# Two products with ones for each norm's sum, root and reciprocal by columns, and a reload spread between products: a decoder layer on one Trainium2 core

## The chip, the cores and the metric

The kernel runs on one core of one Trainium2 chip. Five engines work from queues of their own: TensorE (PE, matrix products into the eight PSUM banks), VectorE (DVE), ScalarE (ACT), GpSimd (POOL) and SyncE (SP, which here issues most DMAs). The metric is the device time of one execution in microseconds (us), a median over runs. The profile calls the loading of weights into PE "PEld".

## The reference

One layer of a hybrid decoder on 1024 prompt tokens and 8 sequences of 4 new tokens (1056 tokens in all), float32, width 1024:

```python
def _rms(x, g):
    return x * lax.rsqrt(jnp.mean(x * x, axis=-1, keepdims=True) + EPS) * g

def _layer(x, p, ...):
    h = _rms(x, n_mix_pre)
    z = h @ w_in                      # q, k, v, pooling input
    a, k_state, v_state = attn_fn(q, k, v)
    m, pool_state = _pool_mixer(u, pool_prev, pos0, w_pool, pool_scale)
    x = x + _rms(concat([a, m]) @ w_out, n_mix_post)
    f = _rms(x, n_ffn_pre)
    f = (silu(f @ w_gate) * (f @ w_up)) @ w_down
    x = x + _rms(f, n_ffn_post)
    x = x + sigmoid(x @ w_ple_gate) * (p @ w_ple)
```

There are four norms per layer. Each needs, for every token, the sum of 1024 squares.

## The kernel before

**Layout.** Activations lie with features on the 128 partitions and tokens along the columns. The 1056 tokens are three groups of N = 352 columns; a half of a group is a tile of 128 x (4 x 352). Every float32 product is made of three single-pass products: each operand is split into a rounded high part and a low part (`split`, L171 to L174: a cast on ACT, then a subtraction on DVE), and high x high, high x low and low x high are added in a PSUM bank. The slots of the pool for activations (30) and of the raw weights (3) are reused; a tile waits until the last reader of its slot is done.

**The norm.** Squares are added over the eight chunks of features into `acc`, 128 x 352. What is left is the sum over the partitions, then 1/sqrt(sum/1024 + eps), and that value on all partitions for the multiplications that follow. `rstd_steps` (L355 to L384) does this twelve times: one pre-mix norm for each group (through `u_norm`, which copies the result to SBUF, L546), two in `ffn_steps` (the norm after mixing and the one before the FFN) for each group, and one in `x2_steps` (after the FFN) for each group. It makes three small products of `acc` with a column of ones (L363, the sums then stand by tokens on partitions), takes root (L365) and reciprocal (L366) of 128 x 3, splits it (L368, L369), multiplies a constant band of identity tiles `diag` by both parts (L375, `dg`) and makes two products with a matrix of ones (L383), which leave the value of each token on all partitions of a PSUM bank.

**The FFN.** Groups 0 and 1 are treated together by a scheme of seven products of half blocks (`seven`, `do_dn_pair`), group 2 directly (`do_one`, `do_dn_one`). The gate and up weights come in slabs of four pairs; the down products of a slab (`do_dn_pair`, two steps j = 0, 1, of seven products with two banks each) add into `accp` on DVE (`ap`, L1226). Group 2's normalised input is used early for the first slabs, then spilled to DRAM (`fsd`), and read back by `do_reload` ahead of the last slab's down products: two halves `fr` by DMA (L1251), each then split into `fh` and `fl`. It is used again from the direct products behind `do_combine`.

**Order.** The program is written by a planner in Python. `STEPS` lists the product steps. Side work such as norms and operand splits is written as generators, which are put on a list with `chain`; each product calls `turn(n)`, n being its matmuls, and `turn` moves the generators on when their time has come. A generator's `yield load, wait` says how many units of DVE work it has just issued (divided by a `share`) and how many units to wait more. `finish` runs generators to their end on the spot. The order of PE is then fixed as written; the order on the other engines is set by a scheduler that follows it. Each engine works through its queue in order.

Of the kernel before, what the change touches and what calls it, by code (L numbers as in the profile page):

```python
# [10 lines left out]
F32 = mybir.dt.float32  # L11
F32R = mybir.dt.float32r
AF = mybir.ActivationFunctionType
ALU = mybir.AluOpType
AX = mybir.AxisListType

P = 128
D = 1024
# [7 lines left out]
N = T // G  # L26
# [1 line left out]
OFF = tuple(N * g for g in range(G + 1))  # L28
NX = N

TB = 3
WIN = 128
NB = SEQ // WIN
PW = (2, 4, 8, 16)
# [28 lines left out]
def trunk_kernel(  # L63
# [32 lines left out]
    nc = tc.nc  # L96
    te, ve, se, ge = nc.tensor, nc.vector, nc.scalar, nc.gpsimd
# [4 lines left out]
    spool = ctx.enter_context(tc.tile_pool(name="spool", bufs=2))  # L102
# [5 lines left out]
    def nm(s):  # L108
        cnt[0] += 1
        return f"{s}{cnt[0]}"  # L110

    def act_tile(shape, dt=F32, s="a"):
        return apool.tile(shape, dt, tag="a", bufs=A_SLOTS, name=nm(s))

    def half(g, dt=F32, s="h"):
        return act_tile([P, 4, NS[g]], dt, s)
# [9 lines left out]
    def mm(*args, **kw):  # L126

        ins = te.matmul(*args, **kw)  # L128
        if pinned[0]:
            tc.keep_in_program_order(ins)  # L130

    def bank():
        return psum.tile([P, 512], F32, tag="b", name=nm("b"))
# [4 lines left out]
    def const(shape, src=None, s="c", dt=F32):  # L138
        t = cpool.tile(shape, dt, name=nm(s))
        if src is not None:  # L140
            nc.scalar.dma_start(t, src)
        return t
# [3 lines left out]
    ident = const([P, P])  # L146
    make_identity(nc, ident)

    diag = const([P, TB, P])
    lap = TB * P - N  # L150
    for i in range(TB - 1):
        ge.tensor_copy(diag[:, i, :], ident)
    ge.memset(diag[:, TB - 1, :], 0.0)
    ge.tensor_copy(diag[:, TB - 1, : P - lap], ident[:, lap:])
    ones = const([P, P])
    ge.memset(ones, 1.0)
    ones_r = const([P, P], dt=F32R)
    ge.tensor_copy(ones_r, ones)
    epst = const([P, 1])
# [7 lines left out]
    def fix(ins):  # L167

        if fixed[0]:
            tc.keep_in_program_order(ins)  # L170

    def split(hi, lo, src):
        fix(se.copy(hi, src))  # L173
        fix(ve.tensor_tensor(lo, src, hi.bitcast(F32), op=ALU.subtract))  # L174
# [140 lines left out]
    def need(k, ahead=LOOK):  # L315

        for i in range(len(made), min(k + ahead + 1, len(ITEMS))):
            kind, js = ITEMS[i]
            if kind == "direct":
                w_split(js[0])  # L320
                made[i] = pairs[js[0]]
            elif kind == "half":
                w_load(js[0])
                hl = two_in_one([P, 4, P])
                split(*hl, raws[js[0]][:, 4:8, :])
                made[i] = hl
            elif kind == "small":
                w_load(js[0])
                hl = two_in_one([P, 2, 256])
                split(*hl, raws[js[0]])  # L330
                made[i] = hl
            else:
                made[i] = w_sums(*(raws[ITEMS[j][1][0]] for j in js))
            for kind, js in ITEMS[i + 1 : i + 3]:
                if kind != "sums":
                    w_load(js[0])
        return made[k]
# [17 lines left out]
    def rstd_steps(acc):  # L355

        n = acc.shape[1]
        sm = bank()  # L360
        for i in range(TB):
            at = min(i * P, n - P)
            mm(sm[:, i : i + 1], acc[:, at : at + P], ones[:, 0:1], start=True, stop=True)  # L363
        sd = spool.tile([P, TB], F32, tag="sd", name=nm("sd"))
        fix(se.activation(sd, sm[:, :TB], AF.Sqrt, bias=epst, scale=1.0 / D))  # L365
        fix(ve.reciprocal(sd, sd))  # L366
        hl = spool.tile([P, 2, TB], F32R, tag="hl", name=nm("hl"))
        fix(ve.tensor_copy(hl[:, 0], sd))  # L368
        fix(ve.tensor_tensor(hl[:, 1], sd, hl[:, 0].bitcast(F32), op=ALU.subtract))  # L369
        dgs = []  # L370
        dg2 = act_tile([P, 2, TB, P], F32R, "dg")
        for h in range(2):
            dg = dg2[:, h]
            fix(
                ve.tensor_tensor(  # L375
                    dg, diag, hl[:, h].bitcast(F32).unsqueeze(2).to_broadcast([P, TB, P]), op=ALU.mult
                )
            )
            dgs.append(dg.rearrange("p i k -> p (i k)"))
        yield 6, 14  # L380
        ps = bank()
        for h in range(2):
            mm(ps[:, :n], ones_r, dgs[h][:, :n], start=h == 0, stop=h == 1)  # L383
        return ps[:, :n]  # L384

    def acc_rows():
        t = act_tile([P, 4, NX], s="acc")
        return [t[:, g, : NS[g]] for g in range(G)]
# [30 lines left out]
    xs, acc1, r1 = [[None] * 2 for _ in range(G)], acc_rows(), [None] * G  # L419
# [77 lines left out]
    n = 4 * NDEC * PST  # L497
# [44 lines left out]
    def u_norm(steps, g):  # L542
        try:
            next(steps)
        except StopIteration as e:
            fix(se.copy(acc1[g], e.value))  # L546
            r1[g] = acc1[g]

    pinned[0] = True
    norms = [None] * G  # L550
# [95 lines left out]
    for c in range(4):  # L646
        n = NDEC * DSEQ
# [67 lines left out]
    def scores(b):  # L715


        t = act_tile([P, 8, WIN])
        cur = [bank() for _ in range(2)]
        prv = [bank() for _ in range(2)] if b else None  # L720
        for c in range(4):
            for which, at in ((cur, b), (prv, b - 1)):
                if which is None:
                    continue
                for kv in range(2):
                    rows = slice(64 * kv, 64 * kv + 64)
                    mm(
                        which[kv][:, c * WIN : (c + 1) * WIN],
                        qT[c][rows, b * WIN : (b + 1) * WIN],
                        kT[rows, at * WIN : (at + 1) * WIN],  # L730
                        start=True,
                        stop=True,
                    )
        for kv in range(2):
            tk = t[:, 4 * kv : 4 * kv + 4, :]
            if b:
                se.copy(tk, v4(prv[kv]))
                ve.copy_predicated(tk, m4(0).bitcast(mybir.dt.int32), v4(cur[kv]))
            else:
                ve.tensor_tensor(tk, v4(cur[kv]), m4(1), op=ALU.add)  # L740
            hs = slice(4 * kv, 4 * kv + 4)
            softmax(tk, 4, 0.125, skp[:, hs], nskp[:, hs])
        return t
# [98 lines left out]
    acc = acc_rows()  # L842
# [46 lines left out]
    t = scores(order[0])  # L889
# [16 lines left out]
    for a, b in zip(order, order[1:] + [None]):  # L906
# [11 lines left out]
        t = t2  # L918
# [10 lines left out]
    fs = [None, None, []]  # L929
# [5 lines left out]
    chains = []  # L935
# [16 lines left out]
    def chain(steps, wait=0, alone=False):  # L952

        chains.append([steps, now[0] + wait, alone])

    def finish(ch_list):
        for ch in ch_list:
            for _ in ch[0]:
                pass
            chains.remove(ch)  # L960
# [40 lines left out]
    def f_operand(src, g):  # L1001
        hi, lo = half(g, F32R, "fh"), half(g, F32R, "fl")
        split(hi, lo, src)
        return hi, lo
# [4 lines left out]
    fsd = [dpool.tile([P, 4, N], F32, name=nm("fsd")) for _ in range(2)]  # L1009
# [190 lines left out]
    accp = {}  # L1200

    def do_dn_pair(s, j, items):
        if j == 0:
            finish(list(chains))
        ia, ib, is_ = items
        for at, which, h, x in (
            (1, ia, 0, "B11"),
            (2, ia, 1, "B21"),
            (4, ib, None, "T4"),
            (6, is_, "S2", "T2"),  # L1210
            (7, is_, "S3", "T3"),
            (5, is_, "S1", "T1"),
            (3, is_, "S4", "B22"),
        ):
            w = need(which)
            w = w if h is None else w[h] if which == is_ else quarter(w, h)
            xh, xl = h7[x]
            if at not in accp:
                accp[at] = half(0, s="ap")
            for r in range(2):  # L1220
                ps = bank()
                gemm(ps[:, :N], [(w[0][:, 2 * c + r, :], w[1][:, 2 * c + r, :], xh[:, c, :], xl[:, c, :]) for c in range(2)])
                turn(6)
                o = accp[at][:, 2 * j + r, :]
                if s:
                    ve.tensor_tensor(o, o, ps[:, :N], op=ALU.add)  # L1226
                else:
                    se.copy(o, ps[:, :N])

    def do_combine():  # L1230
        for a, b in ((2, 1), (1, 6), (7, 1), (1, 5), (1, 3), (4, 7), (7, 5)):
            ve.tensor_tensor(accp[a], accp[a], accp[b], op=ALU.add)
        os_[0] = [accp[2], accp[4]]
        os_[1] = [accp[1], accp[7]]
        for g in (0, 1):
            begun.update((g, m) for m in range(KC))
# [9 lines left out]
            nc.sync.dma_start(d, t)  # L1246

    def do_reload():
        for h in range(2):
            t = half(2, s="fr")  # L1250
            nc.sync.dma_start(t, fsd[h])  # L1251
            fs[2][h] = f_operand(t, 2)

    def do_reload_sums():
        os_[2] = [half(2, s="o") for _ in range(2)]
# [217 lines left out]
```

## Time and profile before

| | us |
|---|---|
| median of 3 runs | 1093.5 |
| lowest and highest | 1092.64, 1093.7 |
| the profiled execution | 1093.79 |
| its span | 1092.0 |
| its mean granted PE clock | 0.996 |

Twelve norms and the reload are spread over the whole span: the pre-mix norms lie before 55 us, the six of `ffn_steps` between 220 and 340, the reload near 820, the norms after the FFN between 880 and 1010. Page part 2 cuts the span into 40 slices of 27.3 us and gives the busy share of each engine in tenths.

```profile
DVE  6777478886878966796598898999899997969973
ACT  7423276674555533345543443344443364445531
PEclk9999999999999999999999999999998999999999
```

A row of a timeline has the start, the time from the start to the end of the last of a group, the engine, line, operation, output and input, size and count; in brackets, how long the engine had been idle and what released it. A row of the grouped view ends with busy time, mean nanoseconds of one, and idle time before them. A row of the waits has the total, the number and the longest.

### The profile page before, as it was taken

The page shows a single profiled execution, that of the slowest core. Times are in us where ns is not written, and L with a number is a line of the kernel's source. Part 1 is how long each engine was busy: PE and PEld are TensorE (multiplying, and loading weights), DVE is VectorE, ACT ScalarE, POOL GpSimd, SP SyncE. Part 2 cuts the span into 40 slices and gives each one's busy share as a digit, 9 for nine tenths or more (in the row PEclk, how much of TensorE's full clock was granted, in tenths as well). Part 3 has the DMA queues.
Part 4 walks back from the last instruction along what each step waited for, and adds up shares of the span by engine and source line. Part 5 has one row for each costly group of instructions (what it writes and reads, how often), then busy time and mean ns, then how long its engine had stood idle before and what let it go on. Part 6 is the DMA issues. An engine that isn't in the chain of part 4 may idle for free.

```text
span 1092.0 us, 17927 instructions
## 1 busy us (share of the span) xinstructions
PE 1080.0 (99%) x6979; PEld 1063.7 (97%) x6979; DVE 874.5 (80%) x1298; ACT 511.4 (47%) x863; POOL 284.4 (26%) x212
## 2 busy tenths in 40 slices
PE   9999999999999999999999999999998999999998
PEld 8999988899999999999999999999998999999998
DVE  6777478886878966796598898999899997969973
ACT  7423276674555533345543443344443364445531
POOL 0073032200000023435445454455442000022400
PEclk9999999999999999999999999999998999999999
DMA  8121311544553432322222212213224545553351
GB/s 295 59 71 39 120 48 40 179 150 136 190 186 131 135 116 77 131 78 78 82 74 83 91 59 94 81 59 115 74 88 179 172 167 213 189 209 130 126 203 60
DMA packets 43573, 131.29 MB, mean 120 GB/s; under 512 B 5060, under 2 KB 15588, under 8 KB 43488
## 3 DMA queue, kind: packets, MB, share of 16 engines
q1 hardware_dynamic: 42160, 128.38, 34.4%
q10 hardware_dynamic: 1328, 1.77, 0.5%
q8 instruction: 55, 0.90, 0.3%
q14 instruction: 30, 0.25, 0.1%
HBM read 114.25 MB, written 15.87 MB: 119 GB/s over the span
## 4 chain that ended last, share of the span: by engine, by line
PE 91%; DVE 4%; DMA 2%; issue 1%; ACT 1%; POOL 1%; SPq 0%; DVEq 0%; POOLq 0%; ACTq 0%
PE b L128 90%; PE b L122 1%; DMA xr<-in_x_dram 1%; DMA a<-in_dmask_dram 1%; POOL wr L1054 1%; DVE sl L174 0%; SPq L402 0%; DVE wl L174 0%; DVE mx L693 0%; ACT xr L436 0%; DVE a L801 0%; ACT wh L173 0%; DVE hf L1129 0%; DVE h L428 0%; ACT h L426 0%
## 5 line engine op out<-in xcount | busy, mean ns | idle before, releaser
L1054 POOL TENSOR_TENSOR wr<-wr,wr 128x512 f32<-128x512 f32 x108 | 175.0, 1636 | 484.3 <-DMA wr<-in_w_gu_dram 217.3
L173 ACT CAST wh<-wr 128x1024 fp32r<-128x1024 f32 (+1 forms) x138 | 142.1, 1031 | 165.7 <-PE b L128 99.4
L174 DVE TENSOR_TENSOR wl<-wr,wh 128x1024 fp32r<-128x1024 f32 (+1 forms) x138 | 169.1, 1226 | 49.1 <-ACT wh L173 33.9
L128 PE MATMUL b<-fh,wh 128*128 128x352 f32 x624 | 201.5, 323 | 0.0
L128 PE MATMUL b<-fl,wh 128*128 128x352 f32 x624 | 199.9, 320 | 0.0
L128 PE MATMUL b<-fh,wl 128*128 128x352 f32 x624 | 199.9, 320 | 0.0
L173 ACT CAST sh<-wr 128x1024 fp32r<-128x1024 f32 x72 | 75.7, 1051 | 139.2 <-POOL wr L1054 131.5
L128 PE MATMUL b<-fh,sh 128*128 128x352 f32 x416 | 134.3, 323 | 0.0
L128 PE MATMUL b<-fl,sh 128*128 128x352 f32 x416 | 133.2, 320 | 0.0
L128 PE MATMUL b<-fh,sl 128*128 128x352 f32 x416 | 133.2, 320 | 0.0
L174 DVE TENSOR_TENSOR sl<-wr,sh 128x1024 fp32r<-128x1024 f32 x72 | 96.1, 1336 | 36.8 <-ACT sh L173 18.5
L128 PEld LDWEIGHTS b<-fl,wh 128*128 128x128 f32 x624 | 117.3, 188 | 0.0
L128 PEld LDWEIGHTS b<-fh,wh 128*128 128x128 f32 x624 | 117.0, 188 | 0.0
L128 PEld LDWEIGHTS b<-fh,wl 128*128 128x128 f32 x624 | 117.0, 188 | 0.0
L128 PE MATMUL b<-h,wh 128*128 128x352 f32 x480 | 104.9, 324 | 0.9 <-ACT h L426 0.7
L128 PE MATMUL b<-hid,wh 128*128 128x352 f32 x416 | 99.5, 322 | 0.0
L128 PEld LDWEIGHTS b<-h,wh 128*128 128x128 f32 x480 | 81.4, 188 | 2.1 <-DVE h L428 1.0
L128 PE MATMUL b<-hp,sh 128*128 128x352 f32 x320 | 78.3, 328 | 4.7 <-DVE ap L1226 4.0
L1054 POOL TENSOR_TENSOR wr<-wr 128x512 f32<-128x512 f32 x36 | 51.0, 1418 | 106.5 <-DVE w L174 106.5
L128 PEld LDWEIGHTS b<-fl,sh 128*128 128x128 f32 x416 | 78.2, 188 | 0.0
L128 PEld LDWEIGHTS b<-fh,sh 128*128 128x128 f32 x416 | 78.0, 188 | 0.0
L128 PEld LDWEIGHTS b<-fh,sl 128*128 128x128 f32 x416 | 77.9, 187 | 0.0
(195 smaller groups left out, 2253.6 us busy)
## 6 DMA issues: line engine op xcount, KB each, us to landing
wr<-in_w_gu_dram SPq DMA_DIRECT2D x88, 512.0 KB, 3.3
wr<-in_w_dn_dram SPq DMA_DIRECT2D x40, 512.0 KB, 3.2
wr<-in_w_pg_dram SPq DMA_DIRECT2D x16, 512.0 KB, 3.5
x<-in_x_dram SPq DMA_DIRECT2D x6, 704.0 KB, 9.6
x1d<-x SPq DMA_DIRECT2D x6, 704.0 KB, 3.5
x<-x1d SPq DMA_DIRECT2D x6, 704.0 KB, 6.3
out_y_dram<-yo SPq DMA_DIRECT2D x24, 176.0 KB, 2.1
wr<-in_w_out_b_dram SPq DMA_DIRECT2D x8, 512.0 KB, 3.5
```

Source lines behind the costliest of these rows:

```text
L122: ins = te.transpose(out, src, ident)
L128: ins = te.matmul(*args, **kw)
L173: fix(se.copy(hi, src))
L174: fix(ve.tensor_tensor(lo, src, hi.bitcast(F32), op=ALU.subtract))
L1054: ge.tensor_tensor(out, a, b, op=op)
```

## The change

`rstd_steps` splits `acc` itself, 128 x 352, into a high and a low part, multiplies both with the matrix of ones, and so has the sum of every token on all partitions; then ACT takes the root over 352 columns from PSUM and DVE the reciprocal in place. The result stands in SBUF, in `acc`. The small products, the band of identities and the copy in `u_norm` go.

`do_reload` becomes a generator on the list: both DMAs at its first step, then one half's split after 50 units and the second 10/share + 30 units later. The call that finished all generators moves from the first of the last down products to `do_combine` (and so for every slab's `do_dn_pair`).

```diff
-    diag = const([P, TB, P])
...
     def rstd_steps(acc):
         n = acc.shape[1]
-        sm = bank()
-        for i in range(TB):
-            at = min(i * P, n - P)
-            mm(sm[:, i : i + 1], acc[:, at : at + P], ones[:, 0:1], start=True, stop=True)
-        sd = spool.tile([P, TB], F32, tag="sd", name=nm("sd"))
-        fix(se.activation(sd, sm[:, :TB], AF.Sqrt, bias=epst, scale=1.0 / D))
-        fix(ve.reciprocal(sd, sd))
-        hl = spool.tile([P, 2, TB], F32R, tag="hl", name=nm("hl"))
-        fix(ve.tensor_copy(hl[:, 0], sd))
-        fix(ve.tensor_tensor(hl[:, 1], sd, hl[:, 0].bitcast(F32), op=ALU.subtract))
-        dgs = []
-        dg2 = act_tile([P, 2, TB, P], F32R, "dg")
-        for h in range(2):
-            dg = dg2[:, h]
-            fix(
-                ve.tensor_tensor(
-                    dg, diag, hl[:, h].bitcast(F32).unsqueeze(2).to_broadcast([P, TB, P]), op=ALU.mult
-                )
-            )
-            dgs.append(dg.rearrange("p i k -> p (i k)"))
-        yield 6, 14
+        hl = act_tile([P, 2, n], F32R, "hl")
+        split(hl[:, 0], hl[:, 1], acc)
+        yield 4, 14
         ps = bank()
         for h in range(2):
-            mm(ps[:, :n], ones_r, dgs[h][:, :n], start=h == 0, stop=h == 1)
-        return ps[:, :n]
+            mm(ps[:, :n], ones_r, hl[:, h], start=h == 0, stop=h == 1)
+        fix(se.activation(acc, ps[:, :n], AF.Sqrt, bias=epst, scale=1.0 / D))
+        fix(ve.reciprocal(acc, acc))
+        return acc
     def u_norm(steps, g):
...
-            fix(se.copy(acc1[g], e.value))
-            r1[g] = acc1[g]
+            r1[g] = e.value
     def do_dn_pair(s, j, items):
-        if j == 0:
-            finish(list(chains))
     def do_combine():
+        finish(list(chains))
     def do_reload():
-        for h in range(2):
-            t = half(2, s="fr")
-            nc.sync.dma_start(t, fsd[h])
-            fs[2][h] = f_operand(t, 2)
+        def steps():
+            ts = [half(2, s="fr") for h in range(2)]
+            for h in range(2):
+                nc.sync.dma_start(ts[h], fsd[h])
+            yield 0, 50
+            for h in range(2):
+                fs[2][h] = f_operand(ts[h], 2)
+                yield 10, 30
+
+        chain(steps())
```

How the rows move, at three places of DVE. The first is the first norm, at the start: `xr` is the input (squares added up into `acc`, and operand `h` split from it), `a` the first products times the norm's value. Before:

```order
L428 SCALAR_TENSOR_TENSOR h_188<-xr_124,c_72,h_187 128x352 x4
L366 RECIPROCAL sd_335<-sd_335 128x3
L368 CAST hl_338<-sd_335 128x3
L369 TENSOR_TENSOR hl_338<-sd_335,hl_338 128x3
L375 TENSOR_TENSOR dg_341<-c_82,hl_338 128x384 x2
L393 TENSOR_TENSOR xr_120<-xr_120,xr_124 128x1408
L394 TENSOR_TENSOR xr_120<-xr_120 128x704
L395 TENSOR_TENSOR acc_104<-xr_120 128x352
L428 SCALAR_TENSOR_TENSOR h_361<-xr_166,c_72,h_360 128x352 x4
L540 TENSOR_TENSOR a_210<-b_218,acc_104 128x352
```

and of the change:

```order
L405 SCALAR_TENSOR_TENSOR h_183<-xr_119,c_72,h_182 128x352 x4
L167 TENSOR_TENSOR hl_326<-acc_99,hl_326 128x352
L370 TENSOR_TENSOR xr_115<-xr_115,xr_119 128x1408
L371 TENSOR_TENSOR xr_115<-xr_115 128x704
L372 TENSOR_TENSOR acc_99<-xr_115 128x352
L405 SCALAR_TENSOR_TENSOR h_346<-xr_161,c_72,h_345 128x352 x4
L360 RECIPROCAL acc_99<-acc_99 128x352
L405 SCALAR_TENSOR_TENSOR h_391<-xr_194,c_72,h_390 128x352
L517 TENSOR_TENSOR a_205<-b_213,acc_99 128x352
```

Ahead of the product one subtraction stands for five operations; the reciprocal has moved behind it.

The second place is group 2's second FFN norm: `y` its scaled input, `fl` the low part of its operand, `wl` those of weights, `sq` squares of another group. Before:

```order
L366 RECIPROCAL sd_2842<-sd_2842 128x3
L368 CAST hl_2845<-sd_2842 128x3
L369 TENSOR_TENSOR hl_2845<-sd_2842,hl_2845 128x3
L375 TENSOR_TENSOR dg_2848<-c_82,hl_2845 128x384 x2
L978 SCALAR_TENSOR_TENSOR y_1287<-x_2512,c_72,b_2889 128x352 x2
L174 TENSOR_TENSOR wl_2882<-wr_2716,wh_2881 128x1024
L850 TENSOR_TENSOR acc_1301<-acc_1301,sq_2878 128x352
L978 SCALAR_TENSOR_TENSOR y_1287<-x_2512,c_72,b_2889 128x352 x2
L978 SCALAR_TENSOR_TENSOR y_1976<-x_2514,c_72,b_2889 128x352 x2
L174 TENSOR_TENSOR wl_2927<-wr_2885,wh_2926 128x1024
L850 TENSOR_TENSOR acc_1301<-acc_1301,sq_2923 128x352
L978 SCALAR_TENSOR_TENSOR y_1976<-x_2514,c_72,b_2889 128x352
```

and of the change, from the reciprocal to the second half's `fl`:

```order
L360 RECIPROCAL acc_1269<-acc_1269 128x352
L954 SCALAR_TENSOR_TENSOR y_1255<-x_2480,c_72,acc_1269 128x352 x4
L826 TENSOR_TENSOR acc_1269<-acc_1269,sq_2875 128x352
L167 TENSOR_TENSOR wl_2879<-wr_2835,wh_2878 128x1024
L167 TENSOR_TENSOR fl_2885<-y_1255,fh_2884 128x1408
L826 TENSOR_TENSOR acc_1269<-acc_1269,sq_2914 128x352
L167 TENSOR_TENSOR wl_2918<-wr_2837,wh_2917 128x1024
L954 SCALAR_TENSOR_TENSOR y_1944<-x_2482,c_72,acc_1269 128x352 x4
L167 TENSOR_TENSOR wl_2959<-wr_2882,wh_2958 128x1024
L826 TENSOR_TENSOR acc_1269<-acc_1269,sq_2955 128x352
L167 TENSOR_TENSOR fl_2965<-y_1944,fh_2964 128x1408
```

The four scalings of each half now stand together, and the reciprocal heads them where it headed the product before.

The third place is the reload: `p` and `u` are the last gate and up products, `hid` the split of what they make, `ap` the down products' additions. Before:

```order
L1081 TENSOR_TENSOR p_8345<-p_8345,b_8456 128x352
L174 TENSOR_TENSOR fl_8477<-fr_8474,fh_8476 128x1408
L1163 TENSOR_TENSOR u_8421<-u_8421,p_8345 128x352
L174 TENSOR_TENSOR wl_8404<-wr_8343,wh_8403 128x1024
L174 TENSOR_TENSOR hid_8337<-u_8421,hid_8337 128x352
L174 TENSOR_TENSOR w_8486<-wr_8388,w_8486 128x512
L1226 TENSOR_TENSOR ap_5196<-ap_5196,b_8491 128x352
L1226 TENSOR_TENSOR ap_5196<-ap_5196,b_8499 128x352
L1226 TENSOR_TENSOR ap_5213<-ap_5213,b_8507 128x352
```

and of the change, starting with the first addition, which follows `p`:

```order
L1200 TENSOR_TENSOR ap_5116<-ap_5116,b_8399 128x352
L1200 TENSOR_TENSOR ap_5116<-ap_5116,b_8411 128x352
L1139 TENSOR_TENSOR u_8341<-u_8341,p_8265 128x352
L1200 TENSOR_TENSOR ap_5133<-ap_5133,b_8419 128x352
L167 TENSOR_TENSOR wl_8324<-wr_8263,wh_8323 128x1024
L167 TENSOR_TENSOR hid_8257<-u_8341,hid_8257 128x352
L167 TENSOR_TENSOR w_8394<-wr_8308,w_8394 128x512
L1200 TENSOR_TENSOR ap_5133<-ap_5133,b_8427 128x352
L1200 TENSOR_TENSOR ap_5164<-ap_5164,b_8449 128x352
L1200 TENSOR_TENSOR ap_5164<-ap_5164,b_8457 128x352
L1200 TENSOR_TENSOR ap_5185<-ap_5185,b_8471 128x352
L1200 TENSOR_TENSOR ap_5185<-ap_5185,b_8479 128x352
```

The first half's `fl` comes behind these eight additions, the second half's eleven DVE rows later. On SP's queue both `fr` loads now stand together, ahead of one `w_dn` load that used to stand between them.

More of the change, by code (lines that the diff above doesn't have):

```diff
@@ L29 @@
 NX = N
-TB = 3
 WIN = 128
@@ L147, in trunk_kernel @@
     make_identity(nc, ident)
-    diag = const([P, TB, P])
[L150 to L154, printed above, removed]
     ones = const([P, P])
```

## The prediction

> **What bounds the kernel now.** I read the page first: the busy times of the engines.
>
> ```profile
> PE 1080.0 (99%) x6979; PEld 1063.7 (97%) x6979; DVE 874.5 (80%) x1298; ACT 511.4 (47%) x863; POOL 284.4 (26%) x212
> ```
>
> TensorE (PE) is busy for 1080.0 of the span's 1092.0 us. A busy engine is the bound only if it waits for nobody, so the next views are the chain that ended last and the waits of PE.
>
> ```profile
> 218.65 564.72 PE b L128 x3567
> ```
> ```profile
> PE b L128 <- DVE ap L1226: 4.0, 1, 4.0
> ```
>
> The chain's longest pieces are unbroken runs of matmuls; this one (start, length) goes from 218.65 to 783.4. There each pass taken off PE shortens the span by its own time, as long as nothing else gets late. Of the few waits, the longest, 4.0 us at once, is for the down products' additions. The windows show its stage and the one behind it (time, PE, PEld, DVE, ACT, POOL, clock, DMA share, GB/s).
>
> ```profile
> 800.00:830.00 30.00, 25.26 (x148) 24.69 (x147) 26.76 (x39) 14.58 (x20) 12.79 (x8) 0.91 0.45 167
> 830.00:900.00 70.00, 70.00 (x438) 70.00 (x438) 65.66 (x98) 32.71 (x47) 0.23 (x1) 0.99 0.47 160
> ```
>
> In the first, PE loses 4.74 of 30 us, the clock falls to 0.91, and VectorE (DVE) is busy for 26.76: locally DVE is the bound. Behind it PE is full again, but DVE has only 4.3 us left in 70.
>
> **Removed: the 72 passes on the ones column.** Each norm issued three fp32 products of 128x1, two passes each; a timeline of PE shows them as one group of six (start, length).
>
> ```profile
> 226.04 0.72 PE L128 MATMUL b<-c,acc 128*128 128x1 f32 x6
> 226.62 0.41 PE L128 MATMUL b<-mh,wh 128*128 128x352 f32 x1
> 226.87 0.33 PE L128 MATMUL b<-ml,wh 128*128 128x352 f32 x1
> 227.04 0.32 PE L128 MATMUL b<-mh,wl 128*128 128x352 f32 x1
> ```
>
> Starts are what counts here, since passes overlap. A 128x352 matmul normally follows the last after 0.16 us (226.87 to 227.04), so without the six passes the `mh` product would have begun at 226.04 and the `ml` product at 226.20. It began at 226.87: the passes cost 0.67 us, and 12 norms cost 12 x 0.67 = 8.0 us. All lie in stretches where PE waits for nothing, except the first. The two products with ones remain, with data of 352 columns where `dg` stood: no change on PE. **Term 1: -8.0 us.**
>
> **Moved: what precedes the two products.** Before, they wait for a root, a reciprocal, a cast, a subtraction and two products with the diagonal; now for a cast and a subtraction over 352 columns. The nearest rows for these are the hidden layer's split.
>
> ```profile
> L173 ACT CAST hid<-sl 128x352 fp32r<-128x352 f32 x22 | 10.6, 482 | 7.5 <-DVE sl L1175 7.3
> L174 DVE TENSOR_TENSOR hid<-sl,hid 128x352 fp32r<-128x352 f32 x22 | 12.5, 569 | 1.7 <-ACT hid L173 1.5
> ```
>
> The only norm on the path is the first one, at the start:
>
> ```profile
> 24.96 1.38 ACT L436 ACTIVATE xr<-xr 128x1408 f32<-128x1408 f32 x1 [1.98 <-DVE h L428]
> 27.71 0.80 PE L128 MATMUL b<-dg,c 128*128 128x352 f32 x2 [0.50 <-DVE dg L375]
> 28.35 1.45 PE L128 MATMUL b<-h,wh 128*128 128x352 f32 x8
> ```
>
> The new cast stands behind the square on ScalarE (ACT), which ends at 26.34: cast until about 26.87, subtraction until about 27.45, the second product at 27.55 and the next `h` at 27.7 where it was at 28.35. So this norm also gains 0.65, its full share; were the cast 1 us later, this one norm would gain nothing and the sum would be 0.65 smaller.
>
> **Added: root and reciprocal over 352 columns, behind the products.** The root follows on ACT, 0.5 us or so by the cast above, where 0.26 was; with it come four more table loads (17 for 13), 1.28 us each on an engine that is 47% busy. The reciprocal has no row of this width. The nearest:
>
> ```profile
> L705 DVE RECIPROCAL sm<-sm 128x1 f32<-128x1 f32 x2 | 0.3, 164 | 0.0
> L705 DVE RECIPROCAL sm<-sm 128x4 f32<-128x4 f32 x16 | 2.7, 171 | 0.2
> L365 ACT ACT_TABLE_LOAD x5 | 6.4, 1283 | 0.1
> ```
> ```profile
> L366 DVE RECIPROCAL sd<-sd x12: 145/169/177, 26.5 to 1007.0; 128x3 f32<-128x3 f32 x12
> ```
>
> Three more columns cost 7 ns, 2.3 ns each, so 352 columns take 164 + 351 x 2.3 = 970 ns; the lower end is another 352-column operation of DVE (the 569 ns above, or somewhat less: 500). For an upper end, the twelve of 128x3 (least, median, most) spread over 32 ns; if all of that hid in three columns, 10.7 each, 352 would take 3.9 us. I take 1.0, since means over 16 are steadier than a spread.
>
> The Trainium skill, "VectorE: DVE Perf Modes", section "Walkthrough: the 8-slice pipeline in each mode", says that the reciprocal iterates its divide with a repeat count of 8. At the 0.96 GHz of that page, 8 cycles per column would be 2.9 us, an estimate; but then 128x4 would stand 25 ns above 128x1, and the rows show 7.
>
> On DVE a norm loses five operations, two of them over 384 columns, and gains two over 352 (0.57 and the 1.0 just taken), so its load hardly moves. What changes is latency behind the product: root and reciprocal now come after it. That is hidden where a norm's user has slack, and one has little: group 2's second FFN norm.
>
> ```profile
> 260.76 1.07 DVE L978 SCALAR_TENSOR_TENSOR y<-x,c,b 128x352 f32<-128x352 f32 x2 [1.98 <-PE b L128]
> ...
> 271.42 1.63 DVE L174 TENSOR_TENSOR fl<-y,fh 128x1408 fp32r<-128x1408 f32 x1
> ```
> ```profile
> 272.00 0.32 PE L128 MATMUL b<-fh,wh 128*128 128x352 f32 x1
> ```
> ```profile
> 273.90 0.32 PE L128 MATMUL b<-fh,wh 128*128 128x352 f32 x1
> ```
>
> Its operands are used at 272.00 (first half) and from 273.90 (second). The last split ended at 273.05, 0.85 us early. Now the scalings start after root and reciprocal: product ready at 260.6, root until 261.5, reciprocal until 262.5. Following the new DVE order (four scalings 2.05, an addition and weight split 1.7, split of the first half 1.6, again 1.7, four scalings 2.05, 1.7, 1.6) the last split ends at about 275.0; 274.6 with a reciprocal of 0.5, 277.9 with one of 3.9. Needed at 274.07, it costs 0.5 to 3.9 us. **Term 2: +0.9 us.** At the other norms PE waits for nothing before the change, and their results are used several weight tiles later.
>
> **Moved: the reload.** This is the 4.0 us wait. The DVE rows and the PE rows around it:
>
> ```profile
> 820.87 0.52 DVE L1081 TENSOR_TENSOR p<-p,b 128x352 f32<-128x352 f32 x1
> 821.30 2.27 DVE L174 TENSOR_TENSOR fl<-fr,fh 128x1408 fp32r<-128x1408 f32 x1
> 823.50 0.51 DVE L1163 TENSOR_TENSOR u<-u,p 128x352 f32<-128x352 f32 x1
> 823.93 1.21 DVE L174 TENSOR_TENSOR wl<-wr,wh 128x1024 fp32r<-128x1024 f32 x1
> 825.07 0.51 DVE L174 TENSOR_TENSOR hid<-u,hid 128x352 fp32r<-128x352 f32 x1
> 825.50 0.68 DVE L174 TENSOR_TENSOR w<-wr,w 128x512 fp32r<-128x512 f32 x1
> 826.11 2.66 DVE L1226 TENSOR_TENSOR ap<-ap,b 128x352 f32<-128x352 f32 x6
> ```
> ```profile
> 821.44 0.58 PE L128 MATMUL b<-hp,sh 128*128 128x352 f32 x2 [0.74 <-DVE p L1081]
> ...
> 822.35 0.32 PE L128 MATMUL b<-hp,sl 128*128 128x352 f32 x1
> 826.67 0.95 PE L128 MATMUL b<-hp,sh 128*128 128x352 f32 x2 [4.00 <-DVE ap L1226]
> ...
> 831.21 0.48 PE L128 MATMUL b<-hp,sh 128*128 128x352 f32 x2
> ```
>
> The first `ap` addition frees a bank. It stands behind 4.7 us of other DVE work. PE lost 0.9 us before 821.44, 4.16 before 826.67 (due at 822.51), and then 2.1: 15 matmuls took 4.54 us until 831.21, where 0.16 each makes 2.4. Together 7.2 us. In the new order two additions follow `p` at once, a third comes before the weight split, and the 2.27 us split comes after eight of them. Replayed with these durations: first addition done at 821.9, third at 823.2, then `wl`, `hid` and `w` (2.2 us), the fourth at 825.9. A bank holds six matmuls, 0.95 us, so PE, due to want the fourth bank at 825.4, waits 0.5 us; the split of 2.0 and the `sl` behind the eighth cost about 0.7 more. The 0.9 stays, since the cast of `fr` still stands ahead of the `hid` cast on ACT. 2.1 remain of 7.2. **Term 3: -5.1 us**, between -7.2 (no stall left) and -3 (two stalls twice as long). The operands' second half comes later, but both are used only at the direct products, behind all down products of both steps.
>
> **Sum.** -8.0 + 0.9 - 5.1 = -12.2, from the profiled execution's 1093.8: 1081.6. It stood 0.3 above the median, so 1081.3. With the outer ends, -8.0 + 0.5 - 7.2 and -8.0 + 3.9 - 3: 1078.8 to 1086.4.
>
> **Rivals.**
> (a) The stall moves instead of shrinking: a new addition waits behind the split of `fr` and PE stands as long as before. For it: DVE is busy for 26.76 of 30 us there. Against it: the additions are spread. Then terms 1 and 2 are left: 1086.4. The Trainium skill, "TensorE: Matmul & The Clock Gate", section "Part 1: The HAM clock gate", halves the clock after an idle window of about 3.4 us; the row at 826.67 agrees, and by it several shorter waits would not repeat the 2.1.
> (b) The wide reciprocal takes 3.9 us. For it: no row of this width. Against: 7 ns for three columns. Term 2 is then 3.9, and the two norms between 830 and 960 put some 3 us more each on a DVE with 4.3 left in the first 70, of which I let 2 reach PE: 1093.5 - 8.0 + 3.9 - 5.1 + 2 = 1086.3.
> (c) Slower than before: both loads of `fr` now stand together on SP's queue, ahead of weight loads.
>
> ```profile
> 816.55 0.33 SPq L183 DMA_DIRECT2D wr<-in_w_dn_dram  x1
> ```
> ```profile
> 821.39 0.42 SPq L1251 DMA_DIRECT2D fr<-fsd  x1
> ```
>
> Before, the second one was issued at 821.39, behind that weight load. If its buffer comes free only then, the weights start 4.9 us late, and PE loses up to 4.9, which alone eats term 3 (about 1086). The kernel gets slower if the buffer is held until 816.55 + 12.2 = 828.8: by 1 us if until 830 (1094.5). Against it: the buffer's last reader is a split of `hf` that ended by 806.10.
>
> ```profile
> 805.30 0.80 DVE hp L174
> ```
>
> **How the numbers follow.** Forecast 0.63; (a) 0.13; (b) 0.11; (c) 0.13, of which 0.08 past the point where it turns slower and 0.03 near no change. The likeliest case has 1078.8 to 1086.4; (a), (b) and the part of (c) in which weights come 5 to 8 us late (up to 1089) extend the range upwards, and 2 us are added below since the replay of the reload is by hand: 1077 to 1089. A difference of under 0.2%, about 2.2 us, can't be told from none by this measurement. Faster by more: 0.63 + 0.13 + 0.11 + 0.02 = 0.89; same 0.03; slower 0.08.
>
> **What would show it.** Term 1: PE's instructions 72 fewer, and no row of `c,acc`. Term 2: a wait of PE for `fl` or `fh` near 271, and the duration of the 128x352 reciprocal. Term 3: waits on `ap` under 1 us each, and a clock near 1.0 in the window that had 0.91. The prediction is wrong if the longest wait on `ap` stays above 3 us, if the reciprocal takes over 2 us, or if the SP queue issues the second `fr` later than the weights' time.

## The result, and the profile after

| | us |
|---|---|
| changed kernel, median of 4 runs | 1100.72 (1099.61 to 1101.55) |
| kernel before, beside it | 1093.6 (1092.64 to 1094.27) |
| ratio, 95% interval | 1.0065, 1.0048 to 1.0083 |
| profiled span, before and after | 1092.0 and 1098.8 |

The change makes the kernel slower by 7 us; the forecast was 12 us faster, and the time lies outside its range. The page's busy times and PE's slices after:

```profile
PE 1080.2 (98%) x6907; PEld 1062.4 (97%) x6907; DVE 888.9 (81%) x1262; ACT 523.5 (48%) x876; POOL 284.6 (26%) x208
...
PE   9999999999999999999999999999999999999898
```

PE has 72 instructions fewer (6907 for 6979), as it should, and the dip near 820 us is gone. Yet it is busy for as long as before, 1080.2 us for 1080.0: the matmuls that are left must take longer together. And it waits more, in more places. The view of PE's waits (total, number, longest):

```profile
PE b L127 <- DVE hl L167: 2.5, 2, 2.1
PE b L127 <- DVE p L1057: 2.3, 2, 2.1
PE b L127 <- DVE ap L1200: 1.7, 2, 1.4
PE b L127 <- DVE u L1057: 1.5, 1, 1.5
PE b L127 <- ACT fh L166: 1.4, 1, 1.4
PE b L127 <- DVE fl L167: 1.3, 1, 1.3
PE b L127 <- DVE wl L167: 1.3, 1, 1.3
```

These are the seven longest of eleven rows. The single wait of 4.0 us for `ap` has become 1.4. In its place stand waits for the norm's own split (`hl`), for group 2's operand (`fh`, `fl`), for a weight split (`wl`) and for additions that free banks (`p`, `u`). All eleven sum to 14.5 us, where the six of before sum to 7.7. The grouped view shows what is new on DVE and ACT:

```profile
L360 DVE RECIPROCAL acc<-acc 128x352 f32<-128x352 f32 x12 | 28.2, 2350 | 3.0 <-ACT acc L359 2.9
L359 ACT ACTIVATE acc<-b,c 128x352 f32<-128x352 f32 x12 | 6.6, 552 | 0.1
L167 DVE TENSOR_TENSOR hl<-acc,hl 128x352 fp32r<-128x352 f32 x12 | 6.2, 523 | 3.1 <-ACT hl L166 3.1
```

The reciprocal takes 2350 ns, not the 1.0 us of the prediction; root and split are as foreseen. How it reaches PE is read best at group 2's second FFN norm, in a timeline of DVE:

```profile
261.84 2.35 DVE L360 RECIPROCAL acc<-acc 128x352 f32<-128x352 f32 x1
264.23 2.07 DVE L954 SCALAR_TENSOR_TENSOR y<-x,c,acc 128x352 f32<-128x352 f32 x4
...
270.93 2.07 DVE L954 SCALAR_TENSOR_TENSOR y<-x,c,acc 128x352 f32<-128x352 f32 x4
...
274.48 1.62 DVE L167 TENSOR_TENSOR fl<-y,fh 128x1408 fp32r<-128x1408 f32 x1
```

and in the timeline of PE:

```profile
274.44 0.43 PE L127 MATMUL b<-fh,wh 128*128 128x352 f32 x1 [1.38 <-ACT fh L166]
276.16 0.66 PE L127 MATMUL b<-fl,wh 128*128 128x352 f32 x1 [1.28 <-DVE fl L167]
276.61 0.49 PE L127 MATMUL b<-fh,wl 128*128 128x352 f32 x1
276.91 0.49 PE L127 MATMUL b<-fh,wh 128*128 128x352 f32 x1
...
279.16 0.32 PE L127 MATMUL b<-fh,wl 128*128 128x352 f32 x1
```

The last split starts at 274.48, after it is due, and PE stands for 1.38 and again for 1.28 us. From 276.61 to 279.16 nine matmuls take 2.55 us, 0.28 each where 0.16 is usual, which costs 1.1 more; the granted clock from 275 to 280 us is 0.66. The Trainium skill, "TensorE: Matmul & The Clock Gate", section "Part 1: The HAM clock gate", says that the clock is halved after an idle window of about 3.4 us. Here two waits of 1.38 and 1.28 us with one matmul between them were enough for half speed. The length of a wait alone does not settle it in this trace: half speed also follows a single wait of 2.06 us that ends at 888.48 (0.70 in the 5 us from 888), and none follows waits of 2.08 and 1.52 us at 1037 and 1041 (1.00 from 1036 to 1042).

The remaining difference is in stretches without any wait. Windows of the kernel before and of the changed one, each within its longest run of matmuls (the number behind PE's busy time is that of matmuls):

```profile
333.00:817.00 484.00, 484.00 (x3048) 483.94 (x3047) 404.54 (x537) 213.65 (x297) 194.99 (x124) 1.00 0.27 90
```
```profile
283.00:824.00 541.00, 541.00 (x3383) 541.00 (x3383) 449.85 (x580) 251.45 (x342) 195.11 (x125) 1.00 0.30 102
```

Both are full at a clock of 1.00, but a matmul follows the last after 484 / 3048 = 158.8 ns before, and after 541 / 3383 = 159.9 ns now. (A window also counts the matmuls that run across its edges; from start to start it is 158.9 and 160.0 ns.) I call this time from start to start the pitch. 1.1 ns on 3383 matmuls are 3.7 us.

So the views account for +6.8 us of span with passes removed -8.0, waits +6.8, and a longer pitch in this run +3.7; 4.3 are left. The starts of all matmuls in the two traces show what they are. From start to start the stalls make +8.8 and not +6.8, since a stall also takes up time in which the matmul before it still counts as busy. The longer pitch makes +4.8 over the whole span, 3.3 of it between 340 and 815 us. Matmuls at half speed make only +0.8, since the kernel before had 1.9 us of that loss behind its own wait of 4.0. About 0.4 stays unexplained.

### The profile page after: what moved, and what is told of

Read it like the earlier page. It is cut to its first block, busy times and chain, and to the rows that moved or that the text cites. A ratio compares the mean times of both kernels' runs of the same rounds, so it can differ in the third digit from the quotient of the medians.

```text
span 1098.8 us, 17750 instructions
## 1 busy us (share of the span) xinstructions
PE 1080.2 (98%) x6907; PEld 1062.4 (97%) x6907; DVE 888.9 (81%) x1262; ACT 523.5 (48%) x876; POOL 284.6 (26%) x208
## 4 chain that ended last, share of the span: by engine, by line
PE 86%; DVE 9%; issue 2%; DMA 1%; POOL 1%; ACT 0%; SPq 0%; DVEq 0%; ACTq 0%; POOLq 0%
PE b L127 85%; DVE wl L167 1%; PE b L121 1%; DVE acc L826 1%; DVE sl L167 1%; DVE ap L1200 1%; DMA a<-in_dmask_dram 1%; DVE ap L1207 1%; POOL wr L1030 0%; DVE fl L167 0%; DVE hp L167 0%; DVE ap L1162 0%; DMA xr<-in_x_dram 0%; DVE x L943 0%; DVE mx L669 0%
## 5 line engine op out<-in xcount | busy, mean ns | idle before, releaser
L127 PE MATMUL b<-fh,wl 128*128 128x352 f32 x624 | 202.5, 325 | 0.0
L167 DVE TENSOR_TENSOR sl<-wr,sh 128x1024 fp32r<-128x1024 f32 x72 | 98.5, 1371 | 38.3 <-ACT sh L166 20.2
```

## Experiments

Every ratio below is to the kernel before, run beside it (medians of 1093.3 to 1093.8 us).

**The two parts alone.** First the reload's edit on the norms of before, then the norms' edit with the reload of before:

```diff
     def do_dn_pair(s, j, items):
-        if j == 0:
-            finish(list(chains))
     def do_combine():
+        finish(list(chains))
     def do_reload():
+        def steps():
...
+        chain(steps())
```

> Only the reload is changed; the norms are those of before. If spreading the reload is worth what its replay said (the 4.0 us wait and the half-speed matmuls behind it go, short waits stay): 1093.6 - 5 = 1088.5 us, with no wait on ap over 1.5 us. Rival (the wait only moves behind the second split): 1092 to 1094. Matmuls should follow each other at the 158.9 ns of before up to the reload in both.

Measured: 1089.9 us, ratio 0.9968 (0.9958 to 0.9979), 3.5 us faster than the kernel before. Its waits:

```profile
PE b L128 <- DVE ap L1224: 1.7, 2, 1.5
```

The 4.0 us wait is gone, 1.5 is the longest left, so the reload's part does what it was to do. The gain is 1.5 us smaller than foreseen, and most of the reason is in windows on both sides of 743 us:

```profile
700.00:740.00 40.00, 40.00 (x254) 40.00 (x253) 35.86 (x48) 18.92 (x26) 18.39 (x12) 1.00 0.22 71
745.00:785.00 40.00, 40.00 (x250) 40.00 (x249) 32.81 (x48) 16.01 (x20) 20.66 (x14) 1.00 0.24 80
```

PE has 254 matmuls in 40 us and then 250, while it is full, at full clock, with the same kind of work. At 743.5 the trace has a pause too short for the view of waits:

```profile
743.14 0.48 PE L128 MATMUL b<-hp,sh 128*128 128x352 f32 x2
743.46 0.32 PE L128 MATMUL b<-hp,sl 128*128 128x352 f32 x1
743.69 0.59 PE L128 MATMUL b<-hp,sh 128*128 128x352 f32 x2
```

One matmul starts 0.23 us behind the last where 0.16 is usual, and the pitch stays longer up to the reload, 70 us on, which costs 1.1 us. This made me suspect that the pitch is something that PE falls into.

> Only the norms are changed; the reload is that of before. If the two parts add up: 1100.7 + 5 = 1105.5 us, with the 4 us wait at the reload back. Rival (the reload's spread is itself a part of the loss after 830 us, where the changed kernel waits at 836, 888, 1037 and 1041): 1101 or less.

Measured: 1103.3 us, ratio 1.0084 (1.0069 to 1.0099), 9.2 us slower than before (1105.5 was foreseen, with 5 us and not 3.5 for the reload). The parts' ratios make 1.0052 together, the change has 1.0065 (1.0048 to 1.0083): they add up within the interval, so the loss comes with the norms' edit. One wait belongs to neither alone: the 2.1 us for `hl` at 888 us in the changed kernel is 0.2 here, and the kernel with the reload alone has none.

**Without the reciprocal.** This leaves out the inverse, and multiplies by the root:

```diff
         fix(se.activation(acc, ps[:, :n], AF.Sqrt, bias=epst, scale=1.0 / D))
-        fix(ve.reciprocal(acc, acc))
         return acc
```

> The changed kernel without its twelve reciprocals of 128x352: it multiplies by the root instead of its inverse, so what it computes is another thing. Theory 1 (the 2.35 us reciprocal, first in DVE's queue, is what makes PE wait at 244, 274, 276, 888, 1037 and 1041): these waits, 9.6 us in all, go, 1091 us, and 1087 if the matmuls also return to 158.9 ns. Theory 2 (the loss is the pitch of the matmuls, 160.0 ns for 158.9, and the waits come from elsewhere): 1098 to 1101.

Measured: 1092.06 us, ratio 0.9986 (0.9976 to 0.9995), 8.7 us less than the changed kernel. The main waits left:

```profile
PE b L127 <- DVE hl L167: 1.9, 2, 1.4
PE b L127 <- DVE ap L1199: 1.7, 2, 1.4
PE b L384 <- POOL c L149: 1.1, 1, 1.1
PE b L127 <- ACT h L402: 1.1, 1, 1.1
PE b L127 <- DVE c L1318: 0.9, 1, 0.9
PE b L127 <- DVE fl L167: 0.5, 1, 0.5
```

The waits for `u`, `fh` and `wl` are gone, and so is the one of 2.1 for `p` at 1037 (0.2 is left for `p`, at the reload); theory 1 holds for these. It does not hold for `hl` (1.4 is left of 2.1): there PE waits, in the changed kernel, for the norm's own split until 888.48, while that norm's reciprocal starts only at 890.87. The pitch of 160.0 ns is unchanged. So the pitch of theory 2 is a second loss beside theory 1's, not a rival to it.

**The pitch.** If it is a pattern that PE takes up at a disturbance, then a product more at a norm should be able to change it. In the changed kernel, at all norms:

```diff
         ps = bank()
+        for _ in range(2):
+            mm(ps[:, :n], ones_r, hl[:, 0], start=True, stop=True)
         for h in range(2):
             mm(ps[:, :n], ones_r, hl[:, h], start=h == 0, stop=h == 1)
```

> The changed kernel with each norm's first product issued two times more ahead of the pair, into the same bank (the value is the same): four products a norm, as two norms together had before at 285 us. Theory 2 (the pitch of the matmuls is a state that PE falls into at the norms' products, by their number): the run between 283 and 824 us leaves 160.0 ns, for 158.9 (631 matmuls in 100 us for 627) it gives 1100.7 + 3.8 - 3.8 = 1100.7 us, for 161.0 it gives 1108. Rival (the pitch hangs on the norm's data or the buffers' places and not on the count): 160.0 ns stay, 24 matmuls cost 3.8 us: 1104.5.

Measured: 1101.9 us (1098.56 to 1105.33), ratio 1.0073 (1.0045 to 1.01). The time alone decides nothing, since the rival's 1104.5 lies within the spread, but the window does (kernel with two more, then the changed one):

```profile
400.00:500.00 100.00, 100.00 (x631) 100.00 (x630) 76.75 (x103) 41.12 (x55) 37.69 (x25) 1.00 0.29 100
```
```profile
400.00:500.00 100.00, 100.00 (x627) 100.00 (x626) 77.72 (x103) 40.66 (x54) 37.73 (x24) 1.00 0.30 103
```

631 matmuls in 100 us as in the kernel before (631 there too), for 627: the pitch has returned. The 24 matmuls more lengthen the profiled span by 1.2 us instead of 3.8. The next runs take fewer, and only in the last norm ahead of the long run; first one product more in the changed kernel (the second argument is the number of products added):

```diff
-        r = yield from rstd_steps(acc[g])
+        r = yield from rstd_steps(acc[g], 1 if g == 1 else 0)
```

> The changed kernel with one product more in that same norm. Theory: the run from 333 to 824 us leaves its 160.0 ns; for 158.9 the time is 1100.7 - 3.4 = 1097.3 us, for 161.1 it is 1104. Rival: 160.0 stays, 1100.9 us.

Measured: 1098.1 us, ratio to before 1.0042 (1.0026 to 1.0058), against 1.0065 (1.0048 to 1.0083) of the changed kernel: 2.5 us less by adding 0.16 us of work. The intervals overlap, so it is again the window that shows the return:

```profile
400.00:500.00 100.00, 100.00 (x632) 100.00 (x631) 77.80 (x104) 40.97 (x57) 38.51 (x25) 1.00 0.30 102
```

In the kernel before, the same edit was to show the opposite:

> The kernel before with one product more (0.16 us) in a single norm, the second FFN norm of group 1, the last ahead of the long run; the value is the same. Theory (the pitch of the matmuls is a state that PE takes at such a disturbance and keeps): the run from 333 to 817 us, some 3000 matmuls, leaves 158.9 ns, for 160.0 the time is 1093.7 + 3.5 = 1097.2 us, for 161.1 it is 1100.5 us. Rival (the pitch belongs to the data, the buffers or the work of other engines): 158.9 stays, 1093.9 us.

> The same with two products more in that one norm. Theory: another state than with none, 1097 or 1100 us, or, if two more lead back to the same, 1094.0 us with a changed pitch only at the norm. Rival: 1094.0 us and 158.9 throughout.

Measured: 1093.85 us, ratio 1.0003 (0.9994 to 1.0013), with one; 1094.81 us, 1.0002 (0.9993 to 1.0012), with two. Both windows have 631 matmuls again: here the rival's numbers came, and the pitch didn't move. So a product more can change the pitch, but it isn't the count alone that sets it; what does is open.

**The removed passes.** Each small product of before issued twice:

```diff
             mm(sm[:, i : i + 1], acc[:, at : at + P], ones[:, 0:1], start=True, stop=True)
+            mm(sm[:, i : i + 1], acc[:, at : at + P], ones[:, 0:1], start=True, stop=True)
```

> The kernel before with each of the three small products with the column of ones issued twice (the same value): 72 passes more. If the passes cost PE 0.67 us a norm, as the prediction's first term has it: 1093.6 + 8.0 = 1101.6 us. Rival (PE has that time to spare, or the following products make up for it): under 1097.

Measured: 1101.99 us, ratio 1.0081 (1.0066 to 1.0096), +8.9 us by the ratio. A timeline shows one norm, with 1.40 us where the six passes of before had 0.72:

```profile
226.68 1.40 PE L128 MATMUL b<-c,acc 128*128 128x1 f32 x12
```

72 passes more cost 7.2 to 10.5 us by the interval, and term 1's 8.0 lies in it. PE's busy time rises by just that, from 1080.0 to 1088.0: PE has no slack for them.

**A version with both repairs.** If the reciprocal is the first loss, one ScalarE function that gives the inverse root in place of root and reciprocal takes it away:

```diff
-        fix(se.activation(acc, ps[:, :n], AF.Sqrt, bias=epst, scale=1.0 / D))
-        fix(ve.reciprocal(acc, acc))
+        fix(se.activation(acc, ps[:, :n], AF.Abs_reciprocal_sqrt, bias=epst, scale=1.0 / D))
```

> The changed kernel with one ScalarE function (the inverse root) in place of root and reciprocal. If the reciprocal's place in DVE's queue is what the waits hang on, this is as the run without it: 1092 us, waits at 244, 274 and 1041 gone, with the right values if the function is good enough. Rival (the function needs more table loads or is slower than the root, and ScalarE becomes late for the operands): 1096 or more. Against the kernel before: 1 to 2 us faster, or the same.

Measured: 1093.94 us, ratio 1.0 (0.9988 to 1.0011): 6.8 us less than the changed kernel, level with the one before, and 1.9 above the run without any inverse (1.5 by the ratios, whose intervals overlap). The waits for `u`, `fh` and `wl` and the long one for `p` are gone as there, but `hl` has grown:

```profile
PE b L127 <- DVE hl L167: 3.0, 2, 2.6
```

With the one product more on top:

> The changed kernel with the inverse root in one ScalarE function, and one product more in the last norm ahead of the long run, as in the run with one product more of the changed kernel. If the state it had there is reached again: 158.9 ns from 348 to 820 us, 1093.9 - 3.4 = 1090.5 us. Rival (other small waits decide the state anew): 160.0 ns, 1094.

Measured: 1089.49 us, ratio 0.9966 (0.9954 to 0.9977): 3.7 us less by the ratios for one added matmul, the pitch back at 631 in 100 us. The traces show 3.6 of it as pitch. Last, the norms after the FFN wait longer between split and products:

```diff
-        r = yield from rstd_steps(acc3[g])
+        r = yield from rstd_steps(acc3[g], gap=34)
```

> The same, and in the norms after the FFN the planner waits 34 units instead of 14 between the split and the two products. If the wait for the split at 885 us (2.6 us) comes from products that stand too early in PE's order behind a full DVE: it goes, 2.5 us less than the run without this, 1088 us. Rival (DVE is that full there that the wait only moves to the operands behind): no difference.

Measured: 1085.83 us, ratio 0.9931 (0.9914 to 0.9947), 3.7 us less than without it, where 2.5 were foreseen; a wait of 0.9 us for `c` at 1034 has gone as well. Near 885 us the products now run without a wait, and PE's busy time on the page is 6.0 us below that of the kernel before:

```profile
PE 1074.0 (99%) x6908; PEld 1057.0 (97%) x6908; DVE 864.5 (80%) x1250; ACT 524.3 (48%) x877; POOL 284.0 (26%) x208
```
```profile
882.93 0.48 PE L127 MATMUL b<-hl,c 128*128 128x352 f32 x2
```

This version beats the kernel before by 7.5 us and the changed one by about 15.

## Why the prediction was wrong

**Term 1 (-8.0) held.** Doubling the passes cost 8.9 us, and 8.0 of PE's busy time.

**Term 3 (-5.1) had the right mechanism and about the right size.** Alone it gave -3.5 (-4.6 to -2.3); a wait of 1.5 us behind the first `fl` stayed, where 0.7 was foreseen, and the pitch took 1.1 more. In the change itself the reload's stage gained 4.4, by the starts of matmuls.

**The reciprocal was mis-sized.** The prediction went from 128x1 and 128x4 to 352 columns by their difference of 7 ns, and chose 1.0 us inside 0.5 to 3.9. The measured 2.35 us is 6.7 ns a column; above the 164 ns of a single column it is 6.2 ns for each further one, where the two small rows gave 2.3. Their difference did not show the cost of a column here. A reciprocal over 2 us was one of the prediction's own signs of being wrong. The Trainium skill's repeat count of 8 ("VectorE: DVE Perf Modes", "Walkthrough: the 8-slice pipeline in each mode") gave an estimate of 2.9 us, which the text set aside for the rows; it was nearer, though the measurement is 0.6 below it. With 2.35 us term 2 would have been 2.3 us instead of 0.9; the waits of 1.38 and 1.28 there are 2.7.

**The step that failed** is the sentence behind term 2: "At the other norms PE waits for nothing before the change, and their results are used several weight tiles later." That PE does not wait at a norm before the change doesn't tell how much slack that norm has. The reciprocal is first in DVE's queue, and what is late next need not be the norm's user. At 243.9 PE waited 1.3 us for a weight split that stands on DVE behind the residual additions of the norm; at 1037 and 1041 it waited 2.1 and 1.5 us for additions that free banks. DVE and PE at these places:

```profile
231.24 2.35 DVE L360 RECIPROCAL acc<-acc 128x352 f32<-128x352 f32 x1
...
242.60 1.23 DVE L167 TENSOR_TENSOR wl<-wr,wh 128x1024 fp32r<-128x1024 f32 x1
...
1030.81 2.51 DVE L1273 TENSOR_TENSOR o<-o,acc 128x1408 f32<-128x1408 f32 x1
1033.24 1.61 DVE L1321 TENSOR_TENSOR yo<-c,xm 128x352 f32<-128x352 f32 x1
1034.78 2.08 DVE L1276 SCALAR_TENSOR_TENSOR x<-o,c,x 128x352 f32<-128x352 f32 x2
1036.78 0.51 DVE L1057 TENSOR_TENSOR p<-p,b 128x352 f32<-128x352 f32 x1
```
```profile
243.88 0.43 PE L127 MATMUL b<-mh,wl 128*128 128x352 f32 x1 [1.28 <-DVE wl L167]
...
1037.35 0.43 PE L127 MATMUL b<-fh,wh 128*128 128x352 f32 x1 [2.08 <-DVE p L1057]
...
1041.04 0.43 PE L127 MATMUL b<-fh,wh 128*128 128x352 f32 x1 [1.52 <-DVE u L1057]
```

`p` frees the bank that PE waits for, behind 6 us of other work, most of it the norm's. Some 3 of these 6 us are rows that run longer than elsewhere in this stage (1.72, 0.52 and 1.07 us), so the reciprocal is not alone in it. But both runs without it, with the root only and with the one-step inverse, lose the waits at 243.9, 1037 and 1041. Rival (b) had this mechanism, but let only 2 us of it reach PE, where 1.3 + 2.1 + 1.5 came in places that it did not look at.

A second cause at the other norms is the split: at 888 the two products stood too early in PE's order for a split that DVE made late, and 34 units of waiting in place of 14 removed that in the version with the one-step inverse.

**Not in the prediction at all** was the pitch. It took every matmul to cost what it cost before. In the long run that is 3.7 us, half the whole loss; one matmul more gave 2.5 us back in the changed kernel and 3.7 with the one-step inverse.

**The sum closes.** Between forecast (-12.2) and measurement (+7.1) lie 19.3 us, of which the two profiled executions account for nearly all. By the starts of matmuls, stalls at the norms behind 215 us make 12.0 (3.1 at group 2's norm, where term 2 had 0.9, and 8.9 at the others, where it had nothing), half speed behind them 2.6, the pitch 4.8, and the reload's smaller gain 0.7; with term 2's 0.9 taken off this is 19.2.

**Rival (a)** (the reload's stall only moves) and **rival (c)** (weights late behind the `fr` loads) are out: the part alone is faster, and no wait for weights stands in its list. In the change SP issues the weight load behind `fr` at 820.42 for 816.55, at a place where PE itself is 4.3 us later than before. What (a) adds, that several shorter waits would not repeat the loss at half speed, held at the reload, but not at 275 and 890 us, where waits of at most 2.1 us were followed by it. The forecast put 0.08 on slower, all of it on (c): the right sign for a reason that did not happen.

## What to carry to other kernels

When work moves off the bound engine to one that is 80% busy, price the longest new instruction by one of its own width, and then ask of each place what stands behind it in that queue; an engine without waits has shown no slack. After a change compare the number of matmuls in equal full windows, not just waits: a pitch that differs by 0.7% everywhere costs as much as a stall of several us. A product should stand in a fixed order behind the split it needs by as much as the splitting engine can be late, which in the norms after the FFN was more than 14 units; 34 were enough, and nothing between was tried.

## What the hardware showed that I had not expected

The same matmul (128x352, three passes per product) follows the last after 158.9, 160.0 or 161.1 ns on average over runs of hundreds (from the starts of consecutive matmuls in the traces), at a granted clock of 1.00. Within each value the single intervals repeat every six matmuls: 161, 162, 156, 161, 155, 159 ns make 158.9 on average in the kernel before, and 159, 157, 162, 159, 161, 162 make 160.0 in the changed one; from 340 to 815 us over 99% of the intervals equal the one six matmuls earlier within 2 ns, across changes of weights and products. One value can hold for hundreds of us, and the changes looked at here stand at a disturbance: at a norm's two products, at a wait, at a pause of 0.07 us (743 us in the kernel with the reload alone). One product more at a norm moved it in two kernels and not in a third. Which disturbance leads to which pattern, and why, is not settled here; no run varied the buffers' addresses, and each kernel has one trace, so it is open whether its other executions have the same pitch.

DVE's operations with their operands in SBUF took longer at times in the last stage: `o<-o,acc` 2.51 us at 1030.8 beside 1.61 for the fastest of `ap<-ap,acc`, and `yo<-c,xm` 1.61 beside 0.52, while POOL worked from 1030.55 to 1035.99. The kernel before read the norm's value from PSUM in this operation and had 1.61 both times, although POOL worked then too (1010.20 to 1014.13). The Trainium skill, "SBUF — State Buffer", section "SBUF: two separate sides", says that a DVE operation with two SBUF inputs and a GpSimd operation that reads SBUF lock each other out for a whole instruction; the trace fits that (one such POOL operation lasts 1.29 us there, and the loss is 0.90), but no run here took POOL's work away.
